# Differential attention in a hybrid trunk: the keys' low parts stored twice above each other

## The chip, the cores and the metric

The kernel runs on one core of a Trainium2 chip. The metric is the device time of one execution in microseconds (us); the median of three runs before the change is 3005.4 us (3001.9 to 3006.97). The trace comes from one further execution of the same kernel, profiled.

## What is computed

The reference is a trunk of two layers over 256 context tokens and 512 latent tokens with 1024 channels. In each layer three mixers (a convolution, differential attention, RWKV-7) work on the same normalised input, are gated, merged and projected; then follows a squared-ReLU MLP. The change touches the attention alone. It has 4 heads; each has two components of 64 channels for queries and keys, and 128 value channels:

```python
def block(qi):
    s = jnp.einsum('bhcqd,bhckd->bhcqk', qi, k).astype(jnp.float32) * scale
    p = jax.nn.softmax(s, axis=-1)
    a = p[:, :, 0] - lam * p[:, :, 1]
    return jnp.einsum('bhqk,bhkd->bhqd', a.astype(v.dtype), v)
```

Latent queries see all 768 keys, context queries the 256 of the context. Context queries are computed in layer 0 only. Queries and keys of latent tokens are rotated (2-D rotary positions) before.

## The kernel before

Everything is laid out with channels on the 128 partitions and tokens along the free dimension. Matrix products are done in fp32r, a type that TensorE takes at one column per step, and so that nothing is lost each operand is split in two: a high part H, rounded to fp32r, and a low part L = x - H. A projection needs three products for each pair of operands (wh with hh and hl, and wl with hh), all on 128 partitions. The helper `product` (L227) issues one product and charges a modelled time for it; that model knows the number of columns, not the number of rows.

The order of the instructions on each engine is fixed when the kernel is built. Each part of the work is a generator ("stream") that yields the engine that it wants next and the modelled time at which its operands are there. `weave` (L283) always runs the stream that can go on first by these times. In the attention stage the streams are the scores of component 0 and 1 (`attn_scores`, L1732, one instance each), the softmax difference (`attn_diff`), the transposes and value products (`attn_values`), the post-processing (`attn_posts`), the loads of the next head (`attn_loads`, L1719), and, between all of these, projection units with their weight loads and splits (tiles wr, wh, wl, results in mmps).

For each head, `rope_load` (L1680) first loads the queries, then the keys: one tile of 128 partitions holds component 0 in partitions 0 to 63 and component 1 in 64 to 127. It rotates the latent part on VectorE, splits it in H and L (ScalarE makes H, VectorE makes L), and then rearranges the halves by DMA copies that POOL issues. The result is three tiles (H, O, L), in the profile aqh, aqo, aql for queries and akh, ako, akl for keys:

- queries: H becomes high of component 0 above low of component 0; O becomes low of component 1 above high of component 1;
- keys: O becomes the high part of component 1 twice, H the high part of component 0 twice; the last copy (H from H) must wait for the two into O, since they read what it overwrites. L stays as made: component 0 in the upper half, component 1 in the lower.

The loads of head h start once both components have issued the first latent score tile of head h - 1 (`asked`).

A score tile (128 queries, up to 768 keys, one component) then takes two products for each stretch of 512 or 256 keys. The first, over 128 partitions, gives high query times high key plus low query times high key in one go (L1746). The second adds high query times low key, over the 64 partitions of its component (`cr`, L1736 and L1747). VectorE takes the maximum of the tile (ast), ScalarE exp of it (ap). Each component has one score tile in PSUM, so the next score of this component starts after that exp.

Of the kernel before, what the change touches and what calls it, by code (L numbers as in the profile page):

```python
# [11 lines left out]
F32R = mybir.dt.float32r  # L12
# [7 lines left out]
P = 128  # L20
# [4 lines left out]
T = NCTX + NLAT  # L25
# [95 lines left out]
class Trunk:  # L121
# [1558 lines left out]
    def rope_load(self, h, which):  # L1680
        pool, V = self.pat, self.V
        d = self.park[f"{which}{h}"]
        c0 = 0 if (which == "k" or self.need_ctx) else NCTX
        yield self.qk_t, "SP"
        x = pool.tile([P, T], F32, tag="aqk", name="aqk", bufs=1)
        H, O, L = (pool.tile([P, T], F32R, tag=f"a{which}{i}", name=f"a{which}{i}", bufs=1 if which + i == "ql" else 2)
                   for i in "hol")
        t = self.load(x[:, c0:T], d[:, c0:T])
        sw = pool.tile([P, NLAT], F32, tag="asw", name="asw", bufs=1)
        for i in range(4):  # L1690
            o = i ^ 1
            t2 = self.load(sw[32 * i:32 * i + 32, :], d[32 * o:32 * o + 32, NCTX:T])
        t = max(t, self.rope_t)
        yield t, "DVE"
        V.tensor_tensor(out=x[:, NCTX:T], in0=x[:, NCTX:T], in1=self.rope[:, 0, :], op=ALU.mult)
        yield max(t, t2), "DVE"
        V.tensor_tensor(out=sw, in0=sw, in1=self.rope[:, 1, :], op=ALU.mult)
        t = V.tensor_tensor(out=x[:, NCTX:T], in0=x[:, NCTX:T], in1=sw, op=ALU.add)
        self.qk_t = t = yield from self.split_steps(x[:, c0:T], H[:, c0:T], L[:, c0:T], t)
        yield t, "SP"  # L1700
        a, b = slice(0, 64), slice(64, P)
        for dst, src in (((O, b), (H, b)), ((H, b), (L, a)), ((O, a), (L, b))) if which == "q" else (
                ((O, b), (H, b)), ((O, a), (H, b)), ((H, b), (H, a))):
            t = self.load(*(y[r, c0:T].bitcast(F32) for y, r in (dst, src)), q=self.nc.gpsimd) + 1.5
        return (H, O, L), t

    def transposed(self, dst, src, n, t):

# [23 lines left out]
    def attn_scores(self, c, items):  # L1732


        pool, V, S = self.pat, self.V, self.S
        cr = slice(64 * c, 64 * c + 64)  # L1736
        for i, (h, (s0, nq, nk), qt) in enumerate(items):
            yield 0.0, "PE", lambda: self.heads[h] is not None
            hd = self.heads[h]
            q, k = hd["q"], hd["k"]  # L1740
            qs = s0 + qt * P
            yield hd["t"], "PE", None, f"scores{c}"
            ps = self.psb[c].tile([P, 1024], F32, tag=f"s{c}", name="sps", bufs=1)
            for kk in range(0, nk, 512):
                m = min(512, nk - kk)
                self.product(ps[:, kk:kk + m], q[c][:, qs:qs + P], k[c][:, kk:kk + m], start=True, stop=False)  # L1746
                e = self.product(ps[:, kk:kk + m], q[c][cr, qs:qs + P], k[2][cr, kk:kk + m], start=False, stop=True)  # L1747
            if s0 == NCTX and qt == 0:
                self.asked[c] = h + 1
            yield e, "DVE", lambda: self.n_diff >= i - 2  # L1750
            if i not in self.soft:
                self.soft[i] = [None, None, pool.tile([P, 8], F32, tag="ast", name="ast", bufs=3)]
            st = self.soft[i][2]
            V.tensor_reduce(out=st[:, c:c + 1], in_=ps[:, 0:nk], axis=AX.X, op=ALU.max)
            t = V.tensor_scalar(out=st[:, 2 + c:3 + c], in0=st[:, c:c + 1], scalar1=-0.125, scalar2=None, op0=ALU.mult)
            yield t, "ACT", lambda: self.n_diff >= i - 1
            x = pool.tile([P, T], F32, tag=f"ap{c}", name=f"ap{c}", bufs=2)
            t = S.activation(out=x[:, 0:nk], in_=ps[:, 0:nk], func=AF.Exp, scale=0.125, bias=st[:, 2 + c:3 + c],
                             accum_out=st[:, 4 + c:5 + c])
            self.free(f"scores{c}", t)  # L1760
            self.soft[i][c] = (x, t)
# [394 lines left out]
```

## Time and profile before

| what | before |
|---|---|
| median of 3 runs | 3005.4 us |
| the profiled execution, its own time | 3005.17 us |
| its span | 3003.4 us |
| TensorE (PE) busy | 95% |
| VectorE (DVE) busy | 68% |
| ScalarE (ACT) busy | 45% |
| GpSimd (POOL) busy | 7% |
| mean granted TensorE clock | 0.974 of full speed |

The span is the time from the first to the last instruction of the profiled execution. "PE" is the stream of matrix products on TensorE, "PEld" the loading of weights into it, which can run beside a product. Busy time of PE is from the modelled start to the modelled end of products, so overlapping products count once, and a product that waits for its own weights counts as busy. What the engine really does per product is therefore read from the distance between starts.

### The profile page before, as it was taken

To read this page: it belongs to the slowest core of one execution; us is meant where nothing else is said; L and a number is where in the kernel's file an instruction comes from. 1 tells how busy PE (TensorE), PEld (TensorE's weight loads), DVE (VectorE), ACT (ScalarE), POOL (GpSimd) and SP (SyncE) were. 2 spreads that over 40 slices of the span, in tenths; PEclk is the share of its full clock that TensorE was granted. 3 is DMA by queue.
4 is the path that set the end of the run, shared out by engine and by line. 5 is a ranking of instruction groups with operands and counts; after the bars stand their busy time and mean duration, and the time that the engine had idled before them with its cause. 6 is when DMAs were issued, how large, how long until landed. Compare 5 with 4: busy or idle time off the path is not lost. (4 is left out here: it accounts for less than half of the span.)

```text
span 3003.4 us, 55335 instructions
## 1 busy us (share of the span) xinstructions
PE 2843.3 (95%) x21847; PEld 2235.6 (74%) x21847; DVE 2043.1 (68%) x4348; ACT 1344.6 (45%) x2602; POOL 218.2 (7%) x205
## 2 busy tenths in 40 slices
PE   8999999999999788999999999999999998999998
PEld 6777777766778677888888777776766556788887
DVE  6767777478879988666333569898894666654445
ACT  4556555455543434432313346555544554433333
POOL 0000001000001232410000000000100000000000
PEclk8999999999999898999999999999999998999999
DMA  5232233243227453455111313222334425422223
GB/s 204 65 78 72 59 87 101 87 136 105 73 74 240 154 176 121 150 189 186 62 63 65 106 58 91 69 85 74 81 109 150 117 64 164 155 85 96 96 96 103
DMA packets 246596, 326.19 MB, mean 109 GB/s; under 512 B 117872, under 2 KB 123648, under 8 KB 246208
## 3 DMA queue, kind: packets, MB, share of 16 engines
q1 hardware_dynamic: 242160, 311.63, 32.6%
q0 software_dynamic: 2560, 9.45, 1.2%
q8 instruction: 172, 2.82, 0.4%
q10 hardware_dynamic: 1616, 1.56, 0.2%
q14 instruction: 88, 0.72, 0.1%
HBM read 266.32 MB, written 47.60 MB: 105 GB/s over the span
## 5 line engine op out<-in xcount | busy, mean ns | idle before, releaser
L228 PE MATMUL mmps<-hh,wh 128*128 128x512 f32 (+1 forms) x2344 | 856.2, 365 | 21.7 <-ACT wh L92 5.0
L228 PE MATMUL mmps<-hh,wl 128*128 128x512 f32 (+1 forms) x2344 | 852.9, 364 | 2.9 <-DVE wl L92 2.8
L228 PE MATMUL mmps<-hl,wh 128*128 128x512 f32 (+1 forms) x2344 | 851.1, 363 | 4.1 <-DVE hl L92 4.0
L92 DVE TENSOR_TENSOR wl<-wr,wh 128x512 fp32r<-128x512 f32 x596 | 436.8, 734 | 457.4 <-ACT wh L92 443.4
L92 ACT ACTIVATE wh<-wr 128x512 fp32r<-128x512 f32 x596 | 374.5, 630 | 683.7 <-PE mmps L228 636.1
L228 PEld LDWEIGHTS mmps<-hh,wh 128*128 128x128 f32 x2344 | 450.7, 192 | 93.3 <-issue 16.6
L228 PEld LDWEIGHTS mmps<-hh,wl 128*128 128x128 f32 x2344 | 449.9, 192 | 76.6 <-issue 9.6
L228 PEld LDWEIGHTS mmps<-hl,wh 128*128 128x128 f32 x2344 | 450.8, 192 | 72.2 <-issue 7.6
L228 PE MATMUL mmps<-ffh,wh 128*128 128x512 f32 (+1 forms) x792 | 279.4, 353 | 2.9 <-ACT ffh L92 2.9
L228 PE MATMUL mmps<-ffl,wh 128*128 128x512 f32 (+1 forms) x792 | 280.7, 354 | 0.2 <-DVE ffl L92 0.2
L228 PE MATMUL mmps<-ffh,wl 128*128 128x512 f32 (+1 forms) x792 | 278.2, 351 | 0.0
L92 DVE SCALAR_TENSOR_TENSOR cacc<-upad,dww,cacc 128x783 f32<-128x783 f32 (+1 forms) x240 | 216.2, 901 | 4.2
L228 PEld LDWEIGHTS mmps<-ffh,wh 128*128 128x128 f32 x792 | 150.1, 189 | 26.1 <-ACT ffh L92 3.3
L228 PEld LDWEIGHTS mmps<-ffl,wh 128*128 128x128 f32 x792 | 150.3, 190 | 21.6 <-DVE ffl L92 0.7
L228 PEld LDWEIGHTS mmps<-ffh,wl 128*128 128x128 f32 x792 | 149.9, 189 | 21.9 <-DVE wl L92 0.4
L92 POOL TENSOR_TENSOR modj<-modw,scb 128x1024 f32<-128x1024 f32 x48 | 125.4, 2613 | 409.8 <-DMA gate<-g 178.8
L92 POOL TENSOR_TENSOR bk<-bk,pc 128x384 f32<-128x384 f32 x64 | 58.0, 936 | 1198.3 <-PE tps L228 1134.7
L92 DVE SCALAR_TENSOR_TENSOR modw<-modw,scb 128x1024 f32<-128x1024 f32 x80 | 103.8, 1298 | 26.4 <-POOL modj L92 20.7
L92 DVE TENSOR_REDUCE ast<-sps 128x1 f32<-128x768 f32 (+1 forms) x80 | 68.0, 849 | 57.5 <-PE sps L228 57.2
L92 DVE SCALAR_TENSOR_TENSOR x<-mmps,mod,x 128x512 f32<-128x512 f32 (+1 forms) x126 | 80.0, 636 | 31.3 <-PE mmps L228 30.1
L92 DVE SCALAR_TENSOR_TENSOR sq<-mmps,rl 128x512 f32<-128x512 f32 x96 | 57.1, 596 | 42.0 <-ACT rl L92 42.0
L92 ACT ACT_TABLE_LOAD x64 | 82.1, 1283 | 2.0 <-PE mmps L228 0.9
(306 smaller groups left out, 4490.4 us busy)
## 6 DMA issues: line engine op xcount, KB each, us to landing
wr<-in_w_dram SPq DMA_DIRECT2D x268, 256.0 KB, 2.5
wr<-in_win_dram SPq DMA_DIRECT2D x236, 256.0 KB, 2.7
modw<-in_modw_dram SPq DMA_DIRECT2D x96, 512.0 KB, 4.0
wr<-in_pw_dram SPq DMA_DIRECT2D x48, 256.0 KB, 2.7
wr<-in_wo_dram SPq DMA_DIRECT2D x44, 256.0 KB, 2.7
g<-stage SPq DMA_DIRECT2D x24, 384.0 KB, 3.4
gate<-g SPq DMA_DIRECT2D x24, 384.0 KB, 3.9
x<-in_xT_dram SPq DMA_DIRECT2D x16, 384.0 KB, 5.1
```

The source lines that it names most:

```text
L92: f(**kw)
L228: self.nc.tensor.matmul(out, lhsT, rhs, **kw)
```

## The change

The keys get a fourth tile M (akm, two buffers). Three copies are added for each head's keys, on POOL's queue among the others: component 1's low part into the lower and into the upper half of M, and component 0's low part into the lower half of L. The last two copies overwrite what others read, so they wait for those. The second product of a score then uses the whole of the query tile and the whole of L (component 0) or M (component 1). With that it also adds low query times low key, which the kernel before leaves out. The queries are prepared as before.

```diff
@@ -1699,10 +1699,11 @@ rope_load
         a, b = slice(0, 64), slice(64, P)
+        M = None if which == "q" else pool.tile([P, T], F32R, tag="akm", name="akm", bufs=2)
         for dst, src in (((O, b), (H, b)), ((H, b), (L, a)), ((O, a), (L, b))) if which == "q" else (
-                ((O, b), (H, b)), ((O, a), (H, b)), ((H, b), (H, a))):
+                ((O, b), (H, b)), ((O, a), (H, b)), ((M, b), (L, b)), ((M, a), (L, b)), ((H, b), (H, a)), ((L, b), (L, a))):
             t = self.load(*(y[r, c0:T].bitcast(F32) for y, r in (dst, src)), q=self.nc.gpsimd) + 1.5
-        return (H, O, L), t
+        return (H, O, L, M), t
@@ -1733,7 +1734,6 @@ attn_scores
-        cr = slice(64 * c, 64 * c + 64)
...
                 self.product(ps[:, kk:kk + m], q[c][:, qs:qs + P], k[c][:, kk:kk + m], start=True, stop=False)
-                e = self.product(ps[:, kk:kk + m], q[c][cr, qs:qs + P], k[2][cr, kk:kk + m], start=False, stop=True)
+                e = self.product(ps[:, kk:kk + m], q[c][:, qs:qs + P], k[2 + c][:, kk:kk + m], start=False, stop=True)
```

## Rows read from the trace of the kernel before

**Rows 1.** The page: busy us (share of the span) x instructions of each engine.
```profile
PE 2843.3 (95%) x21847; PEld 2235.6 (74%) x21847; DVE 2043.1 (68%) x4348; ACT 1344.6 (45%) x2602; POOL 218.2 (7%) x205
```
**Rows 2.** Stretches: length, PE, PEld, DVE, ACT, POOL, clock, DMA; last two: score products alone.
```profile
600.00:870.00 270.00, 256.28 (x1234) 188.41 (x1233) 220.75 (x381) 140.28 (x279) 11.84 (x23) 0.98 0.31 100
650.00:800.00 150.00, 142.61 (x690) 104.85 (x688) 131.82 (x226) 79.65 (x162) 7.73 (x15) 0.98 0.34 106
900.00:950.00 50.00, 50.00 (x286) 43.78 (x285) 47.07 (x60) 16.71 (x28) 4.81 (x2) 1.00 0.81 275
2300.00:2470.00 170.00, 154.57 (x571) 98.87 (x570) 110.12 (x200) 93.11 (x174) 12.39 (x24) 0.94 0.39 116
...
600.00:870.00 270.00, 57.27 (x160) 30.00 (x160) 37.34 (x48) 38.91 (x96) 0.98 0.31 100
650.00:800.00 150.00, 33.58 (x96) 17.76 (x96) 21.30 (x29) 21.73 (x58) 0.98 0.34 106
```
**Rows 3.** Waits, 600 to 870 us: waiter, releaser, total us, times, longest.
```profile
DVE ast L92 <- PE sps L228: 25.6, 30, 4.8
```
**Rows 4.** Waits, 2320 to 2470 us.
```profile
PE atps L240 <- DVE ap L92: 4.0, 2, 2.2
...
DVE ast L92 <- PE sps L228: 31.6, 29, 5.9
```
**Rows 5.** Order of time on PE (start, duration, ...): one score tile.
```profile
629.76 0.39 PE L228 MATMUL sps<-akh,aqh 128*128 128x512 f32 x1
630.08 0.49 PE L228 MATMUL sps<-akl,aqh 64*128 64x512 f32 x1
630.50 0.38 PE L228 MATMUL sps<-akh,aqh 128*128 128x256 f32 x1
630.82 0.38 PE L228 MATMUL sps<-akl,aqh 64*128 64x256 f32 x1
631.13 0.44 PE L240 MATMUL atps<-ident,ap 128*128 128x128 f32 x2
```
**Rows 6.** Order of time: projection products on 128 rows, 256 and 512 columns.
```profile
629.28 0.28 PE L228 MATMUL mmps<-hl,wh 128*128 128x256 f32 x1
629.40 0.28 PE L228 MATMUL mmps<-hh,wl 128*128 128x256 f32 x1
...
2403.67 0.39 PE L228 MATMUL mmps<-hh,wl 128*128 128x512 f32 x1
2403.67 0.19 PEld L228 LDWEIGHTS mmps<-hh,wh 128*128 128x128 f32 x1
2403.90 0.40 PE L228 MATMUL mmps<-hh,wh 128*128 128x512 f32 x1
```
**Rows 7.** Order of time: the first scores of layer 0, with a weight load.
```profile
617.97 0.38 PE L228 MATMUL sps<-akh,aqh 128*128 128x256 f32 x1 [2.88 <-DMA akh<-akh]
618.28 0.18 PEld L228 LDWEIGHTS sps<-akl,aqh 64*128 64x128 f32 x1
...
618.60 0.39 PE L228 MATMUL sps<-ako,aqo 128*128 128x256 f32 x1
```
**Rows 8.** The score tile: one of four kinds of product (ns min/median/max, first and last start).
```profile
L228 PE MATMUL sps<-akl,aqh x72: 379/384/580, 618.3 to 2456.1; 64*128 64x256 f32 x40, 64*128 64x512 f32 x32
```
**Rows 9.** Order of time: the key copies of layer 0's first head.
```profile
608.17 0.95 DVE L92 TENSOR_TENSOR akl<-aqk,akh 128x768 fp32r<-128x768 f32 x1
608.21 1.03 POOL L245 DMA_DIRECT2D ako<-akh  x2 [5.99 <-ACT akh L92]
...
614.36 0.52 POOL L245 DMA_DIRECT2D akh<-akh  x1 [5.12 <-DVE y L92]
```
**Rows 10.** Order of time, layer 1: first scores of heads 1 and 2, a key copy.
```profile
2366.75 0.47 PE L228 MATMUL sps<-akh,aqh 128*128 128x512 f32 x1 [1.38 <-DMA akh<-akh]
...
2394.12 0.52 POOL L245 DMA_DIRECT2D akh<-akh  x1 [3.03 <-DVE akl L92]
...
2400.20 0.40 PE L228 MATMUL sps<-akh,aqh 128*128 128x512 f32 x1
```

## The prediction

> **What bounds the kernel now.** I read the page's first part, then the stretches of the two attention stages, then the waits in them, and last the order of time on TensorE around a few scores. TensorE (PE) is busy 95% of the span, VectorE (DVE) 68% [rows 1]. The chain of waits on the page is no help here, since the stretch that it follows lies behind both attention stages; so what an attention edit is worth must be read from the stages themselves. Layer 0's attention lies between about 600 and 870 us, layer 1's between 2300 and 2470 [rows 2]. In both, PE is busy 95% and 91% of the time, and its waits are few: the longest kind in layer 1 is 4.0 us in total [rows 4]. DVE, by contrast, waits for score products: 25.6 us in the first stage, 31.6 us in the second [rows 3, 4]. So in these stages PE is what the others wait for, though DVE is not far behind in layer 0 (220.75 of 270 us, and 131.82 of 150 us in its middle).
>
> But PE's "busy" there isn't all streaming. The starts of products show it [rows 5]. One latent score tile of one component is four products: 512 keys against all 128 rows, 512 keys against 64 rows, then the same for 256 keys. They start at 629.76, 630.08, 630.50, 630.82, and what follows starts at 631.13: steps of 0.32, 0.42, 0.32 and 0.31, 1.37 us in all. Ordinary projection products, all on 128 rows, step by 0.23 us for 512 columns and 0.12 for 256 [rows 6]. The half-height product isn't long by itself; what is lost is at its two edges. In [rows 7] the weight load of the 64-row product starts at 618.28, the very time at which its product starts (618.29 is the next row of the same view), while in [rows 6] the load of a 128-row product starts at 2403.67, with the product before it, one whole product (0.23 us) ahead. So between 128 and 64 rows, in both directions, the load isn't laid under the running product, and each edge costs about 0.1 to 0.2 us.
>
> **The change, part by part.** *Removed: the edges.* All four products become 128-row ones. By [rows 6] they would take 2 x 0.23 + 2 x 0.12 = 0.70 us in place of 1.37: 0.67 us less. There are 4 heads x 4 latent tiles x 2 components in each of two layers: 64 such groups of four. The context tiles (layer 0 only: 4 heads x 2 tiles x 2 components = 16) have one pair of 256 keys, at 617.97 and 618.60, 0.63 us [rows 7] in place of 0.24: 0.39 less. The count agrees with the tile view: 4 x 64 + 2 x 16 = 288 products, of which one of four equal kinds has 72 [rows 8]. Sum: 64 x 0.67 + 16 x 0.39 = 42.9 + 6.2 = 49.1 us of PE time, 27.6 in layer 0 and 21.4 in layer 1. Bounds of the new step: 1.37 (nothing won, if the load is still not hidden) and 0.70. I take 0.70, since a 128-row product followed by a 128-row one is the nearest row. That both products of a component now have the same weights is worth nothing in this sum, and the low query times low key product that the second now includes costs no column.
>
> Here the Trainium skill speaks against the change. "TensorE: Matmul & The Clock Gate", Part 3, "What overlaps and what doesn't", says that a weight load runs under products in flight only where the row groups differ. By that, products that all use all rows would never hide their loads, the new pairs would step as the old ones, and the sum would be 0. This trace differs: the load at 2403.67 runs under a product on the same 128 rows.
>
> *How much of it gets through.* Layer 0: between 650 and 800 us DVE is busy 131.82 of 150 us. The densest stretch that I found for DVE here is 47.07 of 50 us, 94% [rows 2]; packed as densely, the work of these 150 us takes 140.2 us, so that at most 9.8 can go. 96 of the stage's 160 score products lie there [rows 2], 60% of 27.6 = 16.6 us of PE time; 9.8 of it passes. The other 11.0 lies where DVE has room. Layer 0: 20.8 us. Layer 1: DVE is at 110.12 of 170 us, so capacity isn't the limit; the chain from head to head is. First scores of heads 1 and 2 start at 2366.75 and 2400.20, and the last key copy of head 2 was issued at 2394.12 [rows 10]: loading, rotating and copying the next head's keys fills most of these 33 us, on SyncE, DVE, ScalarE and POOL, each of which also waits in its own queue behind softmax work, which waits for scores. I take two thirds of 21.4, 14.3 us, between none (that chain sets the pace) and all. What is late next: exp and the transposes behind it, for which PE waits 4.0 us today. Together 35.1 us.
>
> *Added: two copies to lay the component-1 low part twice, one for component 0, for each head's keys.* POOL issues the copies in order. Today: two copies of the high part at 608.21, the third at 614.36 when these have landed, first score at 617.97 [rows 9]. With the change, the two new copies wait for the low part (DVE's akl, 608.17 + 0.95), so they are issued at 609.24 and 609.76, behind the first two; POOL has nothing else queued there but the third copy and the new sixth. The second of them, given the 5.63 us that the second high copy took (608.73 to 614.36), has landed at 615.39; then the sixth copy takes the 3.61 us of today's third: 619.00, so 1.03 us later than today. Where DVE makes akl late (the issue at 2394.12 waited for it, [rows 10]), the new copies go out around 2393.8 and 2394.3, and the sixth has landed 5.63 + 3.61 us behind that, near 2403.6, 3.4 us after today's first score. If all eight heads felt it: 7 x 1.03 + 3.4 = 10.6 us. The planner counts the three added copies itself and so puts other products ahead of the first score; without that cover it is the 10.6, with it 0. I take half, 5.3. The upper bound is a whole further round of 5.63 us in each of eight heads, 45 us. The moved bytes (three half tiles per head) I put at 0: these transfers lie beside weight loads with the DMA engines 31% and 39% busy. The extra 6 KB of each partition are put at nothing too: the pool is one that opens and closes with the attention.
>
> *Order.* The planner orders by modelled times, in which the 64-row product costs what a 128-row one does. So its order changes by the three copies alone; I price that at 0, with some 6 us either way.
>
> *Clock.* The granted clock was 0.98 and 0.94 in these stages [rows 2], that is, 11 and 20 us at the lower of the two levels (1.2 GHz). If all of it returned to 2.4 GHz, half of that time, 15 us, would come back; if PE's waits grow, as much may be lost. Value taken: 0.
>
> Sum: 35.1 - 5.3 = 29.8 us less. The profiled execution took 3005.17 us (span 3003.4), the median is 3005.4, so no correction: **2975 us**.
>
> **Rivals.**
> (a) *All of it passes*, and some clock with it: 49.1 us less or a little more, 2949 to 2958, say 2955. For it: PE hardly waits in either stage. Against: DVE's 88% in the middle of layer 0.
> (b) *The next head's keys set the pace of layer 1*, so that nothing passes there: 20.8 - 5.3 = 15.5 less, 2990 (2985 to 2998). For it: the 33 us between first scores, of which 27 lie ahead of the last copy's issue [rows 10]. Against: in-order engines on that chain wait 31.6 us for scores, and these waits shrink.
> (c) *The change doesn't do what it says*: the load stays outside, nothing is removed and the copies stay: 3005.2 + 5.3 = 3010. It is the case of the skill's rule named above. [Rows 6] speak against it.
> (d) *Slower*: the low parts' second round of copies holds back each head's first score, and PE, with what was put ahead of it used up, stands. Price 45 us: 3005.2 - 35.1 + 45 = 3015. It decides the sign from 35.1 / 8 = 4.4 us per head on. For it: the first score waits for the last copy already (2.88 us before 617.97, [rows 7]). Against: 1.03 us by the working above for a head whose akl is in time.
>
> **How the numbers follow.** About 0.2% (6 us) is what a measurement of this kernel can tell from no change. Forecast (2960 to 2985): 0.56. (a): 0.13. (b): 0.17. (c): 0.06. (d): 0.08. Faster is the first three, 0.86; (c) is same, 0.06; (d) is slower, 0.08. The range of 2950 to 2998 holds the forecast, (b) and most of (a), and leaves out (c), (d) and the lowest edge of (a).
>
> **What would show it.** Right: the second product of a score has 128 rows, its load starts one product ahead, and a group of four takes about 0.7 us; DVE's wait for score products falls well below 57 us in the two stages together; the stages are some 16 to 21 and 9 to 14 us shorter, and the stages behind them as long as before. The sixth copy lands about 1 us after today's third. Wrong: steps of 0.3 us that stay; PE's idle time in the two stages growing by more than 15 us, with akh, akl or akm as what ends it (d, b); or a later stage that gives the gain back.

## The result and the profile after

The changed kernel takes 2973.2 us in the median of 4 runs (2965.6 to 2975.8), the one before 3006.2 us in the runs beside it; the ratio is 0.9887, with an interval of 0.9864 to 0.9909. So it is some 34 us faster (27 to 41), where 29.8 were forecast. The profiled execution took 2974.08 us, its span is 2972.3 us.

TensorE's busy time on the page after (columns as in [rows 1]) is 50.1 us below that of [rows 1]; 49.1 were worked out. That these agree to 1 us is luck: another profile of the same kernel (e9_changed_again below) shows 61.6 us less, at a mean granted clock of 0.977 against 0.973 here. The steps between products, further down, are the better evidence. The span fell by 31.1 us, so 19 us of the freed time became idle time.

```profile
PE 2793.2 (94%) x21847; PEld 2226.4 (75%) x21847; DVE 2042.8 (69%) x4348; ACT 1347.6 (45%) x2602; POOL 232.1 (8%) x229
```

The order of time on PE after the change, for one score tile of component 0 and the start of the next, of component 1; [rows 5] answer to the first four lines. The first group of four starts at 623.92 and the next at 624.61: 0.69 us in place of 1.37, with steps of 0.23, 0.23, 0.12 and 0.11.

```profile
623.92 0.40 PE L228 MATMUL sps<-akh,aqh 128*128 128x512 f32 x1
624.15 0.40 PE L228 MATMUL sps<-akl,aqh 128*128 128x512 f32 x1
624.38 0.28 PE L228 MATMUL sps<-akh,aqh 128*128 128x256 f32 x1
624.50 0.27 PE L228 MATMUL sps<-akl,aqh 128*128 128x256 f32 x1
624.61 0.40 PE L228 MATMUL sps<-ako,aqo 128*128 128x512 f32 x1
```

The weight loads of the same tile. The load for the product at 624.15 starts at 623.92, one product ahead; in [rows 7] the load of the second product started with its product.

```profile
623.92 0.19 PEld L228 LDWEIGHTS sps<-akl,aqh 128*128 128x128 f32 x1
624.15 0.19 PEld L228 LDWEIGHTS sps<-akh,aqh 128*128 128x128 f32 x1
```

What DVE waits for in the two attention stages after the change, 617 to 842 us and 2304 to 2431 us (waiter, releaser, total us, times, longest). The 57.2 us of [rows 3, 4] have become 17.4.

```profile
DVE ast L92 <- PE sps L228: 5.8, 5, 3.9
...
DVE ast L92 <- PE sps L228: 11.6, 10, 2.5
```

Where the time went is read from stretches between marks that both kernels have: from the first to the last score product of each layer (the attention), from there to the last product with yc, the convolution's share of the merge, and in layer 0 from there to the first product with ff, the MLP's second half. First the kernel before: length, PE, PEld, DVE, ACT, POOL busy, clock, DMA.

```profile
618.00:850.60 232.60, 223.82 (x1059) 162.84 (x1059) 194.09 (x337) 122.02 (x246) 9.27 (x18) 0.98 0.29 90
850.60:1062.60 212.00, 186.59 (x983) 155.53 (x983) 190.63 (x250) 85.26 (x136) 37.83 (x15) 0.94 0.49 165
1062.60:1231.20 168.60, 151.16 (x808) 128.39 (x807) 130.80 (x209) 75.96 (x137) 55.95 (x21) 0.94 0.44 149
2323.60:2457.80 134.20, 124.13 (x448) 76.33 (x448) 89.14 (x165) 72.78 (x141) 9.27 (x18) 0.95 0.35 103
```

The same stretches of the changed kernel.

```profile
617.80:842.30 224.50, 205.40 (x1096) 166.48 (x1097) 202.90 (x351) 123.47 (x249) 14.17 (x27) 0.96 0.34 105
842.30:1029.60 187.30, 170.60 (x936) 142.17 (x934) 163.39 (x226) 78.46 (x123) 22.74 (x9) 1.00 0.51 170
1029.60:1212.40 182.80, 155.95 (x807) 131.75 (x807) 144.42 (x217) 80.14 (x144) 65.84 (x26) 0.89 0.43 146
2304.50:2430.80 126.30, 109.19 (x473) 78.52 (x472) 91.53 (x173) 78.58 (x148) 13.90 (x27) 0.95 0.46 136
```

Layer 0's attention is only 8.1 us shorter, the merge 24.7 shorter, the stretch behind it 14.2 longer; together 18.6. Layer 1's attention is 7.9 us shorter. This isn't the picture of the prediction, in which each stage gives what its own products save (16 to 21 and 9 to 14 us) and the stages behind stay as long as they were: 37 more products of layer 0 and 25 more of layer 1 now stand inside the attention. PE's idle time in the two attention stages grew by 17.3 us, from 18.9 to 36.2; key copies end only 5.9 us of it, and waits for the softmax have grown beside them (for exp before a score 9.6 us, against 3.3 before). The order has changed, and it takes experiments to part its share from that of the rows and of the copies.

### The profile page after: what moved, and what is told of

The parts are those of the page before. It is cut to its first block, busy times and chain, and to the rows that moved or that the text cites. A ratio compares the mean times of both kernels' runs of the same rounds, so it can differ in the third digit from the quotient of the medians.

```text
span 2972.3 us, 55378 instructions
## 1 busy us (share of the span) xinstructions
PE 2793.2 (94%) x21847; PEld 2226.4 (75%) x21847; DVE 2042.8 (69%) x4348; ACT 1347.6 (45%) x2602; POOL 232.1 (8%) x229
## 5 line engine op out<-in xcount | busy, mean ns | idle before, releaser
L92 DVE TENSOR_TENSOR wl<-wr,wh 128x512 fp32r<-128x512 f32 x596 | 445.6, 749 | 464.7 <-ACT wh L92 447.8
L228 PEld LDWEIGHTS mmps<-ffh,wh 128*128 128x128 f32 x792 | 150.1, 189 | 24.6 <-ACT ffh L92 1.7
L228 PEld LDWEIGHTS mmps<-ffh,wl 128*128 128x128 f32 x792 | 150.0, 189 | 21.6
L92 DVE TENSOR_TENSOR ffl<-sq,ffh 128x768 fp32r<-128x768 f32 (+1 forms) x64 | 56.5, 883 | 45.6 <-ACT ffh L92 45.4
```

What stands on the lines that cost most here:

```text
L92: f(**kw)
L228: self.nc.tensor.matmul(out, lhsT, rhs, **kw)
```

## The experiments

All ratios are against the kernel before, run on the same chip in the same job. "Less" is (1 - ratio) x 3006 us. PE busy is from each one's page. Median and ratio come from several executions, a profile from one of them, so medians needn't differ by what two profiled spans do.

| kernel | products | order | added copies | median us | ratio (interval) | less us | PE busy us |
|---|---|---|---|---|---|---|---|
| changed | 128 rows | new | 3 | 2973.2 | 0.9887 (0.9864-0.9909) | 34 | 2793.2 |
| e1_copies_only | 64 rows | new | 3 | 3017.6 | 1.0037 (1.0022-1.0052) | -11 | 2848.3 |
| e2_old_order | 128 rows | old | 3 | 2975.6 | 0.9891 (0.9871-0.9911) | 33 | 2787.6 |
| e3_no_copies | 128 rows | old | 0 | 2954.0 | 0.9819 (0.9797-0.9841) | 54 | 2781.1 |
| e4_half_grouped | 64 rows, grouped | old | 0 | 2978.7 | 0.9904 (0.9881-0.9927) | 29 | 2816.5 |
| e5_one_more_round | 128 rows | new | 3, in 3 rounds | 2977.8 | 0.9913 (0.9890-0.9937) | 26 | 2782.2 |
| e6_no_second_round | 128 rows | old | 2, in 1 round | 2958.7 | 0.9839 (0.9819-0.9859) | 48 | 2788.2 |
| e7_unread_copies | 128 rows | old | 2, unread | 2955.2 | 0.9830 (0.9810-0.9850) | 51 | 2783.0 |
| e8_new_order_alone | 128 rows | new | 0 | 2961.6 | 0.9840 (0.9814-0.9867) | 48 | 2786.3 |
| e9_changed_again | 128 rows | new | 3 | 2965.8 | 0.9888 (0.9860-0.9916) | 34 | 2781.7 |
| e10_order_again | 128 rows | new | 0 | 2966.1 | 0.9879 (0.9854-0.9904) | 36 | 2788.6 |
| e11_no_copies_again | 128 rows | old | 0 | 2945.2 | 0.9807 (0.9782-0.9831) | 58 | 2777.5 |

### Rows, order and copies apart

**e1_copies_only** keeps everything of the change but the rows of the second product.

```diff
-  e = self.product(ps[...], q[c][:, qs:qs + P], k[2 + c][:, kk:kk + m], start=False, stop=True)
+  e = self.product(ps[...], q[c][64 * c:64 * c + 64, qs:qs + P], k[2 + c][64 * c:64 * c + 64, kk:kk + m], ...)
```

> The changed kernel with its fourth key tile, its six copies and so its order of all engines' instructions, but the second score product is back on 64 rows. Theory (the gain is TensorE time lost at the edges between 128-row and 64-row products): that time comes back, PE busy returns from 2793 to about 2843 us, and the copies' price stays: 3006 + 5 = 3011 us (3003 to 3018). Rival (part of the gain is the new order that the three copies gave the planner): clearly below before, 2995 us or less.

Measured: 3017.6 us, 11 us slower than before (7 to 16), PE busy 2848.3; both near what the theory has. Without the rows the change is a loss; the whole gain, and 11 us more, is the rows'. The rival falls. At 64 rows, copies and order together cost 11 us, where 5.3 were forecast.

**e2_old_order** issues the three copies at the same places of POOL's queue, but behind the planner's back (`nc.gpsimd.dma_start` in place of `self.load`, and t as for the other copies).

> The changed kernel, but the planner is not told of the three added copies: they are issued at the same places of POOL's queue, and all engines keep the order of the kernel before. Theory (edges): PE busy near 2793 us and 2976 us (2968 to 2986), the wait for the last key copy growing by up to 10 us, since nothing is put ahead of the first scores for it. Rival (order): 2990 us or more.

Measured: 2975.6 us, as the theory has it in the time. But PE's wait for key copies grew by 21 us (26.2 against 5.2 before), where up to 10 were expected, so the time came out by a higher cost and a higher gain than forecast. The order isn't what makes the change fast.

**e3_no_copies** is one line of the kernel before.

```diff
-  e = self.product(ps[...], q[c][cr, qs:qs + P], k[2][cr, kk:kk + m], start=False, stop=True)
+  e = self.product(ps[...], q[c][:, qs:qs + P], k[2][:, kk:kk + m], start=False, stop=True)
```

> The kernel before with one edit: the second product takes all 128 rows of the query tile and of the low-part tile as it stands, without any added copy or tile. So the 64 rows that are added multiply low query parts with a wrong key's low part (component 0) or high query parts of nothing that belongs there; the step that it leaves out is the laying of low parts twice. Order as before. Theory (edges, and a price of the copies of 5 us, 0 to 11): PE busy near 2793 us and 2970 us (2960 to 2978). If the copies cost nothing: as e2_old_order within 3 us. Rival (order): 2990 or more.

Measured: 2954.0 us, and 2945.2 in e11_no_copies_again: 54 and 58 us less than before. That is below the band expected, and it corrects two terms at once. First, the edges give all of their 49.1 us and some more, not 35.1. These are the attention stages of e3_no_copies; 232.6 and 134.2 us before have become 209.0 and 109.6, so 23.6 of 27.6 us pass in layer 0, and 24.6 in layer 1, which had 21.4 to give by the prediction's sum:

```profile
616.10:825.10 209.00, 197.14 (x1060) 160.10 (x1061) 190.18 (x335) 121.74 (x246) 9.28 (x18) 0.97 0.33 101
...
2291.50:2401.10 109.60, 99.31 (x449) 72.62 (x448) 86.40 (x165) 71.41 (x139) 9.49 (x18) 0.95 0.43 125
```

More than the sum could pass because the sum left an edge out: the one behind the last 64-row product of a tile, whose cost falls partly on the product that follows. This is the kernel before:

```profile
632.47 0.38 PE L228 MATMUL sps<-akl,aqo 64*128 64x256 f32 x1
632.78 0.39 PE L228 MATMUL mmps<-hh,wl 128*128 128x256 f32 x1
633.00 0.28 PE L228 MATMUL mmps<-hh,wh 128*128 128x256 f32 x1
```

The projection product at 632.78 takes a step of 0.22 us, where 256 columns take 0.12 in [rows 6]. Over the whole trace, 39 products of 512 columns that follow a score have a median step of 0.34 us and 11 of 256 columns 0.22, against 0.23 and 0.12 elsewhere; 17 transposes that follow one have 0.165 against 0.108. In e3_no_copies all of these step as elsewhere. That is 50 x 0.10 + 17 x 0.06, some 6 us, and 55 us of TensorE time in all, beside the 54 and 58 us measured.

Second, the copies cost 21.6 us in the old order (e2 less e3), not 5.3. PE's waits point to it. In e3_no_copies PE waits for a key copy like this:

```profile
PE sps L228 <- DMA akh<-akh: 4.4, 3, 3.4
```

And in e2_old_order, with the copies and nothing placed ahead of the first scores for them:

```profile
PE sps L228 <- DMA akh<-akh: 14.4, 5, 3.8
PE sps L228 <- DMA akl<-akl: 11.8, 6, 3.5
```

26.2 against 4.4 us: 21.8 us of new waiting. That this nearly equals the 21.6 us of the times is chance, since the two profiled executions are 29.4 us apart. The attention stages of e2_old_order show it:

```profile
613.40:830.80 217.40, 198.95 (x1060) 161.06 (x1060) 190.38 (x335) 121.88 (x246) 13.92 (x27) 0.95 0.37 106
...
2304.50:2434.30 129.80, 108.30 (x448) 78.53 (x449) 86.67 (x164) 71.56 (x139) 14.12 (x27) 0.90 0.42 118
```

They are 28.6 us longer than those of e3_no_copies: 17.8 us more of idle time, and 10.8 us more of busy time for the same products, at granted clocks of 0.95 and 0.90 against 0.97 and 0.95. So in these two executions the waits are the larger part of the difference, and a lower clock goes with them; that of e3_no_copies is the fastest of its four, which makes it larger than the 21.6 us.

### What it is about the copies

**e7_unread_copies**: e3_no_copies with the two copies into M between the high copies, which nobody reads. **e6_no_second_round**: e2_old_order with the low parts split by two VectorE operations into the places where they are needed, so that neither low copy waits for another one.

```diff
+  M = pool.tile([P, T], F32R, tag="akm", name="akm", bufs=2)
+  self.nc.vector.tensor_tensor(out=L[a, c0:T], in0=x[a, c0:T], in1=H[a, c0:T], op=ALU.subtract)
+  t = V.tensor_tensor(out=M[b, c0:T], in0=x[b, c0:T], in1=H[b, c0:T], op=ALU.subtract)
...
-  ((M, b), (L, b)), ((M, a), (L, b)), ((H, b), (H, a)), ((L, b), (L, a))
+  ((L, b), (L, a)), ((M, a), (M, b)), ((H, b), (H, a))
```

> e3_no_copies with the two copies into M on POOL's queue between the high copies, planner not told, read by nobody: 128-row products, order of the kernel before, no second round, nobody waits for the copies themselves. Theory (the queue position costs, since the third high copy stands behind copies that wait for akl, and shares the transfer): 2954 + 8 to 10 = 2963 us (2959 to 2968), the wait for akh up from 4.4 to some 14 us. Rival (only what scores read and wait for costs): 2954 within 3 us.

> As e2_old_order (order of the kernel before, planner not told), but the split makes component 1's low part directly in the lower half of M and component 0's in the upper half of L, by two VectorE operations on 64 partitions in place of one on 128; so only two low copies are left and neither waits for another copy. Theory (of e2_old_order's price against e3_no_copies, 21.6 us, the part that is waited for akl, 11.8 us, is the second round, and the part waited for akh, 14.4 against 4.4 us, is POOL's queue, where the third high copy now stands behind copies that wait for the low part): the first part goes, 2966 us (2960 to 2970), with up to 8 us of it eaten by VectorE's eight added operations of 0.95 us. If the queue alone matters: 2972 or more. If the round alone matters: 2958 or less.

Measured: e7 2955.2 us and e6 2958.7 us. The theory of a price shared between the queue and the second round missed on both: the two copies into M by themselves, their place on POOL's queue and their traffic, cost 1 us by the medians and 3 by the ratios (e7, inside its interval), and without the second round most of the price is gone (e6: 5 us by the medians and 6 by the ratios are left of 21.6), although VectorE does eight operations more. PE's wait for akh rose to 9.0 us in e7 without a clear loss of time, so not each microsecond of such a wait counts; and no wait for akl or akm is left in e6:

```profile
PE sps L228 <- DMA akh<-akh: 7.5, 5, 4.3
```

So in the old order most of the price is the round: the copy that lays component 0's low part double may only start when the two into M have landed. In e2_old_order POOL stands before it in seven of eight heads:

```profile
POOL akl L1705 <- DMA akm<-akl: 13.0, 7, 2.8
```

In the changed kernel a copy into M took 2.4 to 6.1 us from issue to landing, 4.4 in the median of 16. One thing isn't parted: neither e6 nor e7 has a third low copy, so what that copy costs without the wait wasn't run.

### What the price is in the changed kernel

In the changed kernel PE waits only 5.9 us for key copies (akl 3.4, akh 2.5), and yet it is 19 us above e3_no_copies. **e5_one_more_round** makes the last copies later by a further round; **e8_new_order_alone** has the new order without any of the three copies.

```diff
- ((M, a), (L, b))
+ ((M, a), (M, b))
```

> The changed kernel with one source swapped: the copy into the upper half of M reads the lower half of M, which the copy before has just written, in place of the lower half of L. Same bytes, same number of copies, same order on every engine; the last copies of each head's keys come one more round (some 5 us) later. Theory (the copies' price of some 20 us is lateness of the keys): 12 to 25 us above the changed kernel, 2985 to 2998 us, and TensorE's waits for akl and akh grow by as much. Rival (in the changed kernel's order the lateness is covered, and its price is the order alone): within 5 us of 2973.

> The changed kernel's order of all engines' instructions, with none of its three added copies: the planner is charged for them, but they aren't issued, and the second product takes the whole of L as it was made, as in e3_no_copies (so it leaves out the laying of low parts twice). e3_no_copies differs from it by the order alone, the changed kernel by the copies alone. Theory (in the changed kernel the copies' price of some 19 us is the order that they brought, since one more round of lateness cost it only about 5 us): 2970 us (2966 to 2976). Rival (the price is the lateness of the keys in this order too): 2954 us (2948 to 2959).

> The changed kernel as it is, on one chip with the next two, to part its price against e3_no_copies (some 19 us) in order and lateness more sharply than runs on different chips do. Theory (both count): 2973 us (2967 to 2979).

> e8_new_order_alone again (the changed kernel's order, the three added copies left out). Theory (order some 8 us, lateness some 12): 2962 us, between its two neighbours and at least 5 us from each. If the order alone counts: within 4 us of the changed kernel; if lateness alone: within 4 us of the next.

> e3_no_copies again (order of the kernel before, no added copies). Theory: 2954 us (2948 to 2960).

Measured: one more round costs 4.6 us by the medians and 8 by the ratios, and its interval overlaps the changed kernel's. PE's waits for key copies are 12.7 us, 6.8 more than in the changed kernel, while POOL waits 30.9 us for the added round: the theory's 12 to 25 us falls, and the new order covers most of the lateness. e8 came out between its neighbours, at 2961.6 us, which settled nothing. e9 and e11 came out 1 and 3 us below what was expected, e10 0.3 us from the changed kernel, where the theory had at least 5. On one chip side by side, the new order without copies took 2966.1 us, the changed kernel 2965.8, and the old order without copies 2945.2. So most of the price is the order: 21 us here, and 14 us by the mean of both pairs of ratios (0.9860 against 0.9813). Its size is known only roughly: the first pair, e8 against e3, gives 6 us by the ratios, and e8 and e10, one kernel, lie 12 us apart by theirs. What is left to lateness is 0 us here and 8 by those means; that remainder isn't settled.

The stretches of e10_order_again show how an order costs. They have the shape of the changed kernel's, without its copies: layer 0's attention 223.1, the merge 187.8, the stretch behind it 183.5, layer 1's attention 123.8 us.

```profile
621.40:844.50 223.10, 203.98 (x1097) 165.40 (x1097) 202.92 (x351) 123.49 (x249) 9.28 (x18) 0.96 0.32 98
844.50:1032.30 187.80, 173.74 (x936) 144.37 (x935) 161.84 (x227) 78.61 (x123) 22.56 (x9) 0.98 0.50 170
1032.30:1215.80 183.50, 154.91 (x806) 130.89 (x806) 143.07 (x215) 79.87 (x144) 65.62 (x26) 0.89 0.42 144
2303.70:2427.50 123.80, 107.64 (x473) 78.87 (x473) 92.04 (x173) 78.04 (x148) 9.27 (x18) 0.94 0.40 123
```

To bridge the modelled 1.6 us of copies (three of 0.55 us in `load`) the planner pulled products, and splits on DVE, out of the merge into the attention (1097 products against 1060 in e3_no_copies, 202.9 us of DVE against 190.2), and work from behind into the merge's place. The three stretches of layer 0 sum to 594.4 us, against 586.1 in e3_no_copies (209.0 + 210.3 + 166.8); in the last of them the granted clock was 0.89, against 0.95 there. Layer 1's attention is 14.2 us longer than in e3_no_copies, of which its merge gives 3.7 back (104.1 against 107.8 us). In e8, the same kernel, layer 0's stretches sum to 588.3 us and layer 1's attention is 13.6 us longer, so it is layer 1's loss that repeats. PE's waits in layer 0's attention show what the pulled work does, first e10, then e3_no_copies:

```profile
PE mmps L228 <- DVE wl L92: 6.5, 2, 6.4
PE sps L228 <- ACT ap L92: 4.6, 3, 3.4
...
PE sps L228 <- ACT ap L92: 0.8, 3, 0.3
```

PE stands once for 6.4 us at a projection product whose weights DVE hasn't split yet, and longer for exp (ap); in layer 1 the wait for exp is 7.9 us against 3.3. How these waits and the clock add up to the 14 to 21 us isn't shown.

### The edges by themselves

**e4_half_grouped** keeps 64 rows and changes only the sequence of a tile's four products.

```diff
-  for kk in range(0, nk, 512):
-      self.product(... q[c][:, ...], k[c][:, ...], start=True, stop=False)
-      e = self.product(... q[c][cr, ...], k[2][cr, ...], start=False, stop=True)
+  for half in (False, True):
+      for kk in range(0, nk, 512):
+          r, kt = (cr, k[2]) if half else (slice(0, P), k[c])
+          e = self.product(... q[c][r, ...], kt[r, ...], start=not half, stop=half)
```

> The kernel before with the four products of a score tile in another sequence: both 128-row products first, then both 64-row ones, so that two of four edges per tile of 768 keys are gone, and nothing else. Theory (each change between 128 and 64 rows costs, two 64-row products in a row don't): steps near 0.23, 0.32, 0.23, 0.31, a group of four 1.09 in place of 1.37 us, 64 x 0.28 = 18 us of PE time, of which about 0.63 passes: 2995 us (2990 to 3000). Rival (a weight load is hidden only if the rows differ from those in use, or a 64-row product never hides its load): the step between the two 64-row products stays at 0.42, 6 us of PE time at most: 3002 us or more.

Measured: 2978.7 us, 29 us less where 11 were expected, and below the band. The order of time on PE (two products of a kind are merged into one line, x2):

```profile
625.97 0.51 PE L228 MATMUL sps<-akh,aqh 128*128 128x512 f32 x2
626.41 0.29 PEld L228 LDWEIGHTS sps<-akl,aqh 64*128 64x128 f32 x2 [0.25 <-issue]
626.41 0.61 PE L228 MATMUL sps<-akl,aqh 64*128 64x512 f32 x2
626.96 0.20 PEld L240 LDWEIGHTS atps<-ident,ap 128*128 128x128 f32 x2 [0.25 <-issue]
```

The two 128-row products take 0.44 us together, the two 64-row ones 0.55: 0.99 in place of 1.37, 0.38 less and not 0.28. 64 x 0.38 = 24 us; PE busy fell by 26.8. Each change of height costs 0.19 us by this: two of four are gone. It agrees with the kernel before, where a group of four lost 0.67 us and the product behind it another 0.10, 0.77 for four changes. And the 0.55 us of the 64-row pair is 0.20 over the 0.35 that full height takes. A single 64-row product with a change at each end loses as much already ([rows 5]: 0.42 in place of 0.23, 0.31 in place of 0.12), so nothing is left for the load between the two: it is hidden. The rival falls: it isn't the height of the product that costs but the change of height. (Both products of a height have the same weights here; that full-height products hide the load of other weights is in [rows 6], for two 64-row products it wasn't run.)

## Why the prediction was right

Right in the mechanism of the edges, and right in sum by two errors that cancelled:

- *The edges*, 49.1 us of PE time: the mechanism is right, and the size of what was counted too (a group of four takes 0.69 us, 0.70 worked out). The sum ends at the start of the product behind a group and so leaves out the edge there, some 6 us; 55 us is the whole. PE busy fell by 50.1 us, and by 62 and 66 in e3_no_copies and e11. There the mean granted clocks of 0.978 and 0.979, against 0.974, put by estimate 26 to 32 us fewer at the lower level (1.2 GHz), half of which, 13 to 16 us, is enough for the 7 to 11 us over 55.
- *Rival (c)*, the load stays outside: out, since the steps fell from 1.37 to 0.69 us. The rule of the Trainium skill ("TensorE: Matmul & The Clock Gate", Part 3, "What overlaps and what doesn't"), that a load is hidden only behind products on other row groups, doesn't hold here: the load for the product at 624.15 starts at 623.92, under a product on the same 128 rows, and the 64-row pair of e4 goes against it as well.
- *How much gets through*, 35.1 us: the mis-sized term. It is 54 and 58 us in the kernels with nothing else changed, that is, all of it. In layer 0 the cap from DVE was applied to a window of 150 us, as if its work had to stay there. For the whole stage the same 94% would have allowed 26 us (194.09 / 0.94 = 206.5 of 232.6); 23.6 passed, with DVE at 91%. In layer 1 the chain from head to head was taken to hold back a third. It held back nothing: 24.6 us passed there. That it shrank because it waits for scores at several places (DVE 31.6 us, [rows 4]; 12.0 us in e3_no_copies) fits this, but wasn't tested by itself.
- *The copies*, 5.3 us: the other mis-sized term; with the order that they bring they cost 19 to 21 us in both orders. The working had the mechanism: the second round, the one head whose low part comes late, and the 10.6 us if nothing covers it. It halved this, and even the 10.6 was too low by half: without cover (e2) PE's waits for key copies grew by 21.8 us, 2.7 us for each head where 1.03 was taken for seven of eight, and the copies into M waited for DVE's akl five times, not once.
- *The order*, priced at 0 with 6 us either way: that is where most of the copies' price lies in the changed kernel, 14 us by the mean of two pairs that gave 6 and 21.
- *Rival (d)*, its mechanism: real, at 21.6 us where nothing covers it (e2), short of the 35.1 from which it would have decided the sign, and further short of the 54 that pass.

So the time was forecast within 2 us with the gain 19 us too low and the cost 14 to 16 us too low, which is luck. The kernel that beats both is e3_no_copies: the old layout of the low parts, read over all 128 rows. Its added rows multiply, in both components, low query parts with the other component's low key parts; how large that term is in the scores wasn't measured. Whoever wants the term right takes e6_no_second_round, at 2958.7 us.

## What to carry to other kernels

Read what a product costs from the distance between starts, not from its duration: a stream that changes between full-height and half-height products pays at every change, and grouping equal heights, or making all full-height, gets it back. Before adding copies to feed a wider product, ask whether what already lies in those rows will do (in e3_no_copies it adds a wrong term, which must be small enough), and whether the copies can be made without one that waits for another. In a kernel whose order is planned from modelled times, a few modelled microseconds can cost more through the order than through the wait: hide the edit from the planner to see which it is.

## What was not expected of the hardware

A change between 128-row and 64-row products cost about 0.19 us each time (0.77 us for four in the kernel before, 0.38 for the two that e4 takes out), and part of it, 0.10 us, falls on the product behind the change, also where that one is an ordinary projection product. Two 64-row products in a row, on the same rows, cost no such time between them: 0.55 us for 512 and 256 columns, which is the 0.35 of full height and the 0.20 that a single 64-row product between two changes loses too. And two added half-tile copies for each head's keys that nobody reads cost nothing measurable by their traffic and their place on POOL's queue (1 to 3 us, e7), while three of which one must wait for the others cost 21.6 us (e2).
